# RWKV transposes, inverse levels, chain outputs, softmax and tables in larger steps, and the sample tokens of all eight RWKV heads in one go

## The chip, the cores and the metric

One core of one Trainium2 chip runs the kernel. The metric is the device time of one execution in microseconds (us). Engines are named as in the profile: PE is TensorE (PEld its weight loads), DVE is VectorE, ACT is ScalarE, POOL is GpSimd and SP is SyncE, which here only starts DMAs.

## The reference, cut to what matters

One inference step of one decoder layer for 256 prompt tokens and 32 sample tokens (8 sequences of 4), so 288 tokens (NT) of width 2048, all in float32:

```
h = RMSNorm_pre(x);  [p_rwkv | lru_x | lru_gate | q | k | v] = h @ W_in
y = concat(RWKV7(p_rwkv), RGLRU(lru_x, lru_gate), DilatedWindowAttn(q, k, v)) @ W_out
x = x + RMSNorm_post(y)
x = x + RMSNorm_post2(relu(RMSNorm_pre2(x) @ W1)^2 @ W2)
```

RWKV7 has 8 heads of 64 features; per token `S = S*w + (S·(-kk))(kk*a)^T + v k^T`, `y = S·r`, and behind it a normalisation over each head (here `gen_gn`), a bonus term and a gate. RG-LRU is a gated linear recurrence over 512 features. Attention has 8 heads of 128; the sample tokens attend to a cache of 2048 positions, of which the dilated windows use 896 (keys `kc`, values `vc`). Outputs are the new x of all tokens, the RWKV states, the shift rows, the LRU states and the new keys and values.

## The kernel before, in words

**The main matmuls.** W_in is 46 tiles of 128 columns, each against 16 blocks of 128 features; W_out is 16x16 such blocks, and W1 and W2 of the feed-forward part (FFN) 64x16 each. A product with a 128x128 block is `mm3` (L428): three matmuls of 128x128 weights against 288 columns, high part by high part (L429), high by the low part of x (L430), low part of the weight by high (L431). That makes 9120 of them, called *mains* here, and a position in the program is given as the number of mains before it. Weights come as chunks of 512 KB (8 blocks, 24 mains) on SP's queue; ACT writes the high part into `ring_h` (L393), DVE the low part into `ring_l` (L394), and each ring has 3 places.

**The side work.** Everything else (RWKV, LRU, attention) is written as Python generators that are advanced a bit after each chunk (`pump`, with a budget of some us of estimated PE time), so their matmuls and transposes stand in small *batches* between the mains of W_in and W_out. A `yield` ends a step; each engine then runs its instructions in the order in which a scheduler sets them, and it is this order that the change moves. Small matmuls write one of five PSUM banks (`bt`) that are asked for with `bk(n)`. Temporary tiles come from an arena (`aw`, tiles named `ar` and `arx` in the trace), as soon as a place is free.

**RWKV** works on halves `hf` of 4 heads: decay and key preparation (`gen_rwkv`), transposes to token rows (`gen_tok`, L791), products within chunks of 64 tokens (`gen_form`, L815), a triangular inverse by levels (`gen_inv` on DVE, L855/L857, and `gen_mats` once for each 128 tokens `j`: L898, L911, L912, and L928 behind it), the chain over chunks (`gen_chain`: L964, L975, L986, L987, L1002, L1003, L1013), the sample tokens (`gen_rwkv_sample(hf)`, L1049 to L1123), and the normalisation (`gen_gn`: L1138, L1145, two reciprocals L1150, L1151, L1154, L1156, gate L1161), which waits for chain and sample of its half.

**Attention.** `gen_tables` makes bias tables (L1356), `gen_sample_scores` multiplies queries with cached keys (L1409; query tiles by POOL in L1390 and L1393; loads of 896 KB in L1377), softmax is on DVE (L1434), its transposes are L1447, and `gen_sample_pv` multiplies with cached values (L1496, one batch of 28 matmuls of 128x32 weights for each of 2x8 pairs; loads of 1024 and 768 KB in L1474; copies out by L1503). `gen_prompt_attn` (L1547, bias loads by POOL; L1567, L1588) does the prompt. Key and value loads go into *streams*: buffers for one load each, on POOL's queue, in the order in which POOL's instructions stand. Two streams lie in `arm`; `more_streams` adds up to two from the arena once the second RWKV half has its tiles.

Of the kernel before, what the change touches and what calls it, by code (L numbers as in the profile page):

```python
# [311 lines left out]
def build(tc, A, O):  # L312
    nc = tc.nc
    sy, dv, ac, po, pe = nc.sync, nc.vector, nc.scalar, nc.gpsimd, nc.tensor
    with ExitStack() as ctx:
# [227 lines left out]
        lora = arena.get(2, 512)  # L543
# [22 lines left out]
        def gen_prenorm():  # L566
# [12 lines left out]
            sy.dma_start(out=lora, in_=A["lora"].rearrange("p (a b) -> p a b", a=2))  # L579
# [81 lines left out]
        def gen_rwkv(hf):  # L661
# [6 lines left out]
            for f in range(2):  # L668
# [3 lines left out]
                pe.matmul(out=b0[:, :NT], lhsT=lora[0:64, 0, fs], rhs=mw[0:64], start=True, stop=True)  # L672
                pe.matmul(out=b1[:, :NT], lhsT=lora[64:128, 0, fs], rhs=mw[64:128], start=True, stop=True)
# [3 lines left out]
                yield 1.0  # L677
            half_up(LW, -0.5 * CDEC)
# [59 lines left out]
            gens.append(gen_tok(R, "B", BK[:, 0]))  # L738
            gens.append(gen_tok(R, "K", BK[:, 1]))
# [27 lines left out]
            gens.append(gen_tok(R, "V", MV))  # L767
# [6 lines left out]
            gens.append(gen_rwkv_sample(hf, SC, Vs))  # L774
# [11 lines left out]
        def gen_tok(R, name, src):  # L786
            for j in range(2):
                t = yield from aw(256, top=True)
                b, = yield from bk(1)
                for f in range(2):  # L790
                    pe.transpose(b[:, 128 * f:128 * f + 128], src[:, f, 128 * j:128 * j + 128], ident)  # L791
                ac.activation(out=t, in_=b[:, 0:256], func=AF.Copy)
                banks.put(b)
                R[name + str(j)] = t
                yield 0.25
# [79 lines left out]
        def gen_mats(hf, j):  # L875
            R = RS[hf]
            while "MA%d" % j not in R:
                yield 0
            MT = R["MA%d" % j]
            i64 = cbv("i64")  # L880
            i64b = i64.unsqueeze(1).to_broadcast([128, 4, 64])
# [4 lines left out]

            rc = (slice(0, 64), slice(64, 128))
            XT = yield from aw(4, 64, top=True)
            Gp = yield from aw(4, 64, top=True)
            dv.tensor_tensor(out=XT, in0=MT[:, :, 0], in1=lvl(4), op=ALU.mult)  # L890
# [136 lines left out]
        def gen_rwkv_sample(hf, SC, Vs):  # L1027
            R = RS[hf]
            AR, BK, PS = SC[:, 0], SC[:, 1], R["PS"]
            while "Q0" not in R:  # L1030
                yield 0
# [821 lines left out]
```

## Time and profile before

| | before |
|---|---|
| median of 3 runs | 1447.4 us (1447.09 to 1448.56) |
| profiled execution, its time | 1447.71 us |
| its span | 1445.6 us |
| mean granted TensorE clock | 0.989 |
| PE busy | 1412.0 us (98%) |
| DVE busy | 836.5 us (58%) |
| ACT busy | 600.2 us (42%) |
| POOL busy | 63.3 us (4%) |
| DMA | 276.62 MB, mean 191 GB/s |

W_in and W_out with all side work fill the first 600 us, the FFN the rest. Of the chain of work that ended last, 82% is PE, 7% issue, 6% DMA, 4% DVE and 1% POOL. PE is busy nearly throughout, so its average over the span says little of single stretches; they are read one by one.

### The profile page before, as it was taken

The numbers are of one execution on the slowest core, as the hardware profiler recorded it, in microseconds if no ns is written. First come the engines' busy times: TensorE is split into PE (matmuls) and PEld (weight loads), VectorE is DVE, ScalarE is ACT, GpSimd is POOL, SyncE is SP. The second block draws the span as 40 slices with busy tenths as digits, with TensorE's granted clock in tenths as the row PEclk, the third lists the DMA queues.
The fourth block names the chain that finished last, engine by engine and source line by source line (L and its number), as shares of the span: only waits on it lengthen the run. The fifth ranks groups of instructions, "written<-read, shape, count | busy, mean of one in ns | idle before, by whom it ended". The sixth has DMA issues, their size and how long they took to land.

```text
span 1445.6 us, 27979 instructions
## 1 busy us (share of the span) xinstructions
PE 1412.0 (98%) x11730; PEld 1340.2 (93%) x11730; DVE 836.5 (58%) x1431; ACT 600.2 (42%) x870; POOL 63.3 (4%) x127
## 2 busy tenths in 40 slices
PE   8999999899999999999999999999999999999995
PEld 8899778777878999999999999999999999999995
DVE  7796476645686756795533455544455444555555
ACT  7433422333352533664433344333344333444442
POOL 2101010210001100000000000000000000000000
PEclk9999999999999999999999999999999999999998
DMA  8546566676678774344444444444444445444442
GB/s 299 181 152 209 187 240 239 223 271 241 217 292 331 290 286 162 131 148 161 170 164 165 170 162 163 172 161 167 169 161 165 171 161 169 167 161 165 171 162 79
DMA packets 86047, 276.62 MB, mean 191 GB/s; under 512 B 22385, under 2 KB 26017, under 8 KB 83873
## 3 DMA queue, kind: packets, MB, share of 16 engines
q1 hardware_dynamic: 75136, 212.23, 42.6%
q0 software_dynamic: 9920, 60.83, 11.2%
q8 instruction: 92, 1.51, 0.4%
q10 hardware_dynamic: 864, 1.77, 0.4%
q14 instruction: 35, 0.28, 0.1%
HBM read 267.97 MB, written 6.84 MB: 190 GB/s over the span
## 4 chain that ended last, share of the span: by engine, by line
PE 82%; issue 7%; DMA 6%; DVE 4%; POOL 1%; ACT 0%; SPq 0%; POOLq 0%; DVEq 0%; ACTq 0%
PE mm L429 25%; PE mm L431 25%; PE mm L430 25%; DMA arm<-in_vc 2%; DMA arm<-in_kc 2%; PE bt L1409 1%; DVE ring_l L394 1%; PE bt L1496 1%; DMA ar<-in_vc 1%; DMA w<-in_w_in 0%; DVE arm L1830 0%; DMA do<-ar 0%; DVE arx L1831 0%; DVE hl L548 0%; PE bt L898 0%
## 5 line engine op out<-in xcount | busy, mean ns | idle before, releaser
L394 DVE TENSOR_TENSOR ring_l<-w,ring_h 128x1024 fp32r<-128x1024 f32 (+1 forms) x382 | 464.9, 1218 | 385.2 <-ACT ring_h L393 382.7
L393 ACT ACTIVATE ring_h<-w 128x1024 fp32r<-128x1024 f32 (+1 forms) x382 | 402.6, 1055 | 587.2 <-PE mm L430 538.9
L429 PE MATMUL mm<-hh,ring_h 128*128 128x288 f32 x1984 | 599.4, 302 | 4.6 <-ACT ring_h L393 2.8
L431 PE MATMUL mm<-hh,ring_l 128*128 128x288 f32 x1984 | 591.9, 299 | 1.3 <-DVE ring_l L394 1.3
L430 PE MATMUL mm<-hl,ring_h 128*128 128x288 f32 x1984 | 592.9, 299 | 0.0
L429 PEld LDWEIGHTS mm<-hh,ring_h 128*128 128x128 f32 x1984 | 373.6, 188 | 20.1 <-issue 11.8
L431 PEld LDWEIGHTS mm<-hh,ring_l 128*128 128x128 f32 x1984 | 374.9, 189 | 9.7 <-issue 4.3
L430 PEld LDWEIGHTS mm<-hl,ring_h 128*128 128x128 f32 x1984 | 374.6, 189 | 6.4 <-issue 3.5
L430 PE MATMUL mm<-fl,ring_h 128*128 128x288 f32 x1024 | 302.1, 295 | 0.0
L431 PE MATMUL mm<-fh,ring_l 128*128 128x288 f32 x1024 | 301.8, 295 | 0.0
L429 PE MATMUL mm<-fh,ring_h 128*128 128x288 f32 x1024 | 300.3, 293 | 0.0
L429 PEld LDWEIGHTS mm<-fh,ring_h 128*128 128x128 f32 x1024 | 192.5, 188 | 0.0
L430 PEld LDWEIGHTS mm<-fl,ring_h 128*128 128x128 f32 x1024 | 192.5, 188 | 0.0
L431 PEld LDWEIGHTS mm<-fh,ring_l 128*128 128x128 f32 x1024 | 192.4, 188 | 0.0
L1798 ACT ACTIVATE fh<-ft 128x288 fp32r<-128x288 f32 x64 | 28.3, 445 | 78.9 <-DVE ft L1797 78.9
L1806 DVE TENSOR_TENSOR arm<-mm,arm 128x288 f32<-128x288 f32 x48 | 22.0, 458 | 51.1 <-PE mm L431 51.1
L1799 DVE TENSOR_TENSOR fl<-ft,fh 128x288 fp32r<-128x288 f32 x64 | 29.2, 458 | 29.1 <-ACT fh L1798 29.1
L1409 PE MATMUL bt<-arm,ar 128*32 128x448 f32 x256 | 27.8, 546 | 1.7 <-DMA arm<-in_kc 1.7
L1797 DVE SCALAR_TENSOR_TENSOR ft<-mm,rt 128x288 f32<-128x288 f32 x63 | 28.3, 450 | 0.0
L1496 PE MATMUL bt<-arm,ar 128*32 128x128 f32 x648 | 22.6, 287 | 3.5 <-DMA arm<-in_vc 3.5
L1796 ACT ACTIVATE rt<-mm 128x288 f32<-128x288 f32 x63 | 24.9, 395 | 0.4 <-PE mm L431 0.4
L1496 PEld LDWEIGHTS bt<-arm,ar 128*32 128x32 f32 x648 | 17.8, 114 | 6.6 <-DVE ar L1290 3.7
(394 smaller groups left out, 898.6 us busy)
## 6 DMA issues: line engine op xcount, KB each, us to landing
w<-in_w SPq DMA_DIRECT2D x256, 512.0 KB
w<-in_w_in SPq DMA_DIRECT2D x91, 512.0 KB
arm<-in_kc POOLq DMA_DIRECT2D x32, 896.0 KB, 6.1
w<-in_w_out SPq DMA_DIRECT2D x32, 512.0 KB
arm<-in_vc POOLq DMA_DIRECT2D x15, 1024.0 KB, 6.8
ar<-in_vc POOLq DMA_DIRECT2D x9, 768.0 KB, 9.5
arm<-in_vc POOLq DMA_DIRECT2D x7, 768.0 KB, 7.0
arx<-in_xT SPq DMA_DIRECT2D x6, 576.0 KB
```

Of the source, the lines that this page charges most:

```text
L393: ac.activation(out=h[:, lo:hi], in_=t[:, lo:hi], func=AF.Copy)
L394: dv.tensor_tensor(out=l[:, lo:hi], in0=t[:, lo:hi], in1=h[:, lo:hi].bitcast(F32), op=ALU.subtract)
L429: pe.matmul(out=ps, lhsT=h, rhs=xh, start=start, stop=False)
L430: pe.matmul(out=ps, lhsT=h, rhs=xl, start=False, stop=False)
L431: pe.matmul(out=ps, lhsT=l, rhs=xh, start=False, stop=stop)
L1409: pe.matmul(out=bh[32 * h:32 * h + 32, 0:448], lhsT=qz[:, h, b], rhs=t[:, h], start=(b == 0), stop=(b == NB - 1))
L1496: pe.matmul(out=bb[32 * h:32 * h + 32, 0:128], lhsT=PT[:, kt, 32 * h:32 * h + 32], rhs=t[:, q, h], start=(kt == 0), stop=(kt == 6))
L1796: ac.activation(out=r, in_=ps, func=AF.Relu)
L1797: dv.scalar_tensor_tensor(out=f, in0=ps, scalar=0.0, in1=r, op0=ALU.max, op1=ALU.mult)
L1798: ac.activation(out=fh[:, m], in_=f, func=AF.Copy)
L1799: dv.tensor_tensor(out=fl[:, m], in0=f, in1=fh[:, m].bitcast(F32), op=ALU.subtract)
L1806: dv.tensor_tensor(out=facc[:, m], in0=ps, in1=facc[:, m], op=ALU.add)
```

## The change

- `gen_tok` transposes both 128-token blocks of a tile into one bank, and B and K in one step with two banks.
- `gen_mats` handles both blocks `j` at once: 8 groups to a bank, so 16 matmuls of 64x64 (or 32, L924 and L925) stand together, with copies and DVE operations of 512 columns.
- In `gen_chain` the products into `bZ` (L1013) move up to those into `be` (L964), and are now L984 and L978; ACT copies them to Y at once, and DVE adds the rest later.
- `gen_rwkv_sample` runs once, for 4 feature tiles (8 heads), after both halves. So both calls of `gen_gn` wait for the same sample step.
- Tables and softmax transposes take two banks in one step.
- The streams in `arm` shrink from 2304 to 2048 columns; the 512 columns left become a third piece of the arena. Some tiles are freed earlier (`lora_in`, `mw`, `AR`, `PC`), and the LRU outputs become four tiles. `gen_lru` now stands first in the list.

```diff
-        arena = Arena([arx, ar1])
+        arena = Arena([arx, ar1, arm[:, 4096:4608]])
-        streams = [arm[:, 0:2304], arm[:, 2304:4608]]
+        streams = [arm[:, 0:2048], arm[:, 2048:4096]]
...
-            gens.append(gen_tok(R, "B", BK[:, 0]))
-            gens.append(gen_tok(R, "K", BK[:, 1]))
+            gens.append(gen_tok(R, ("B", BK[:, 0]), ("K", BK[:, 1])))
...
-            gens.append(gen_rwkv_sample(hf, SC, Vs))
+            R["SC"], R["Vs"] = SC, Vs
+            if hf:
+                gens.append(gen_rwkv_sample())
...
+            bs = yield from bk(len(pairs))
+            for i, ((name, src), b) in enumerate(zip(pairs, bs)):
+                for j in range(2):
+                    for f in range(2):
+                        o = 256 * j + 128 * f
+                        pe.transpose(b[:, o:o + 128], src[:, f, 128 * j:128 * j + 128], ident)
...
-        def gen_mats(hf, j):
+        def gen_mats(hf):
...
             for l in range(4, 6):
                 b, = yield from bk(1)
-                for h in range(4):
+                for h in range(8):
                     for r in rc:
-                        pe.matmul(out=v4(b)[r, h], lhsT=XT[r, h], rhs=T[r, h], start=True, stop=True)
-                dv.tensor_tensor(out=Gp, in0=v4(b), in1=i64b, op=ALU.add)
+                        pe.matmul(out=v8(b)[r, h], lhsT=XT[r, h], rhs=T[r, h], start=True, stop=True)
+                dv.tensor_tensor(out=Gp, in0=v8(b), in1=i64b, op=ALU.add)
...
-                for h in range(4):
+                for h in range(8):
                     for r in rc:
                         if l < 5:
-                            pe.matmul(out=v4(bT)[r, h], lhsT=Q[r, h], rhs=Gp[r, h], start=True, stop=True)
-                        pe.matmul(out=v4(bQ)[r, h], lhsT=Gp[r, h], rhs=Q[r, h], start=True, stop=True)
+                            pe.matmul(out=v8(bT)[r, h], lhsT=Q[r, h], rhs=Gp[r, h], start=True, stop=True)
+                        pe.matmul(out=v8(bQ)[r, h], lhsT=Gp[r, h], rhs=Q[r, h], start=True, stop=True)
...
+                    bZ, = yield from bk(1)
+                    for f in range(2):
+                        for e in range(2):
+                            re = slice(64 * e, 64 * e + 64)
+                            pe.matmul(out=bZ[re, 64 * f:64 * f + 64], lhsT=Z[re, f], rhs=AR[re, 1, f, tok],
+                                      start=True, stop=True)
...
+                    ac.activation(out=Y[:, :, tok], in_=v2(bZ), func=AF.Copy)
...
-        def gen_rwkv_sample(hf, SC, Vs):
+        def gen_rwkv_sample():
+
+            while not all("Q0" in R and "SC" in R for R in RS):
+                yield 0
...
-            while "Y" not in R:
+            while not all("Y" in R for R in RS):
                 yield 0
             b, = yield from bk(1)
-            for f in range(2):
+            for f in range(4):
...
+            for hf in range(2):
+                ac.activation(out=RS[hf]["Y"][:, :, tk], in_=v4(b, 32)[:, 2 * hf:2 * hf + 2], func=AF.Copy)
+                RS[hf]["Ys"] = True
...
             for g in range(2):
-                for lo, n in ((0, 464), (464, 464)):
-                    b, = yield from bk(1)
+                bs = yield from bk(2)
+                for b, lo, n in ((bs[0], 0, 464), (bs[1], 464, 464)):
...
-        gens += [gen_tables(), gen_lora()]
+        gens += [gen_lru(), gen_tables(), gen_lora()]
         for hf in range(2):
-            gens += [gen_rwkv(hf), gen_form(hf), gen_inv(hf), gen_mats(hf, 0), gen_mats(hf, 1), gen_chain(hf), gen_gn(hf)]
-        gens += [gen_lru()]
+            gens += [gen_rwkv(hf), gen_form(hf), gen_inv(hf), gen_mats(hf), gen_chain(hf), gen_gn(hf)]
```

**PE, the last inverse level of the first half.** Around main 916 of the kernel before, the two token blocks have a batch of 8 each at L912:

```order
L429 MATMUL mm<-hh,ring_h 128x288
L912 MATMUL bt<-ar_88 64x64 x8
L430 MATMUL mm<-hl,ring_h 128x288
L431 MATMUL mm<-hh,ring_l 128x288
L429 MATMUL mm<-hh,ring_h 128x288
L430 MATMUL mm<-hl,ring_h 128x288
L912 MATMUL bt<-ar_88 64x64 x8
L431 MATMUL mm<-hh,ring_l 128x288
```

In the changed kernel, around main 908, the same work (now L925) and what follows it (L928, now L940, beside key matmuls L1438) read:

```order
L430 MATMUL mm<-hl,ring_h 128x288
L925 MATMUL bt<-ar_88 64x64 x16
L431 MATMUL mm<-hh,ring_l 128x288
L429 MATMUL mm<-hh,ring_h 128x288
L430 MATMUL mm<-hl,ring_h 128x288
L431 MATMUL mm<-hh,ring_l 128x288
L429 MATMUL mm<-hh,ring_h 128x288
L430 MATMUL mm<-hl,ring_h 128x288
L1438 MATMUL bt<-arm,ar_88 32x448 x8
L940 MATMUL bt<-ar_88 64x64 x16
```

Two batches of 8 became one of 16, with the same matmuls in it. In all, PE has 198 small batches before and 162 after, of which 118 and 92 hold tiles smaller than 128x128.

**DVE, the normalisation.** In the kernel before, the first half's reciprocals (L1150) stand behind the low part of a weight chunk (L394), among the inversion steps of the second half (L855, L857) and the sample state (L1121, L1123):

```order
L394 TENSOR_TENSOR ring_l<-w_2306,ring_h 128x1024
L1150 RECIPROCAL ar_88<-ar_88 128x288
L855 TENSOR_TENSOR ar_88<-ar_88 64x1
L1121 TENSOR_TENSOR ar_88<-bt,ar_88 128x512
L857 TENSOR_REDUCE ar_88<-ar_88 64x1
L1150 RECIPROCAL ar_88<-ar_88 128x288
L855 TENSOR_TENSOR ar_88<-ar_88 64x4
L1123 TENSOR_TENSOR ar_88<-ar_88 128x512
L857 TENSOR_REDUCE ar_88<-ar_88 64x2
L1151 TENSOR_TENSOR ar_88<-ar_88 128x576
```

In the changed kernel nothing of `gen_gn` stands there. It stands near main 1900, between the low parts of two successive chunks (L1177 is the reciprocal, L1178, L1181 and L1183 the operations behind it, L1148 and L1149 the sample state, L1528 a copy of attention, L1210 and L1211 of an LRU input). The first part of it:

```order
L394 TENSOR_TENSOR ring_l<-w_3863,ring_h 128x1024
L1166 SCALAR_TENSOR_TENSOR ar_88<-bt,ar_88 128x288
L1303 SCALAR_TENSOR_TENSOR ar_88<-ar_88 128x288
L1210 TENSOR_TENSOR arx<-mm,rs_in 128x256
L1211 TENSOR_TENSOR arx<-mm,rs_in 128x32
L1177 RECIPROCAL ar_88<-ar_88 128x288 x3
L1178 TENSOR_TENSOR ar_88<-ar_88 128x576
L1528 SCALAR_TENSOR_TENSOR arx<-bt,ca,arx 128x128
```

and what follows directly, up to the next low part:

```order
L1181 TENSOR_SCALAR ar_88<-ar_88,pv 128x288 x2
L1177 RECIPROCAL ar_88<-ar_88 128x288
L1183 TENSOR_TENSOR ar_88<-ar_88 128x576
L1178 TENSOR_TENSOR ar_88<-ar_88 128x576
L1148 TENSOR_TENSOR ar_88<-bt,ar_88 128x512
L1181 TENSOR_SCALAR ar_88<-ar_88,pv 128x288 x2
L1149 TENSOR_TENSOR ar_88<-ar_88,arm 128x512
L1183 TENSOR_TENSOR ar_88<-ar_88 128x576
L1148 TENSOR_TENSOR ar_88<-bt,ar_88 128x512
L394 TENSOR_TENSOR ring_l<-w_3943,ring_h 128x1024
```

Both halves' normalisations, four reciprocals, now stand in one stretch between two low parts.

**POOL, the value loads.** In the kernel before, the first value loads of the run (L1474) go to the two `arm` streams in turn, and an arena tile (`ar`) joins late:

```order
L1474 DMA arm<-in_vc 128x2048
L1474 DMA arm<-in_vc 128x1536
L1474 DMA arm<-in_vc 128x2048
L1474 DMA arm<-in_vc 128x1536
L1474 DMA ar_88<-in_vc 128x2048
L1474 DMA arm<-in_vc 128x2048
L1474 DMA arm<-in_vc 128x1536 x2
```

In the changed kernel the same loads (L1499) go round four streams from their start:

```order
L1499 DMA arm<-in_vc 128x1536
L1499 DMA ar_88<-in_vc 128x2048
L1499 DMA arx<-in_vc 128x1536
L1499 DMA arm<-in_vc 128x2048
L1499 DMA arm<-in_vc 128x1536
L1499 DMA ar_88<-in_vc 128x2048
L1499 DMA arx<-in_vc 128x1536
L1499 DMA arm<-in_vc 128x2048
```

A load into a stream waits for the batch that read the load four places before, no longer two.

## Rows read from the trace of the kernel before

**Rows 1.** Windows: busy us (count) per engine, granted clock, DMA share, GB/s.
```profile
0.00:600.40 600.40, 584.32 (x5519) 513.60 (x5520) 409.90 (x919) 250.57 (x403) 63.32 (x127) 0.99 0.66 236
609.50:1428.00 818.50, 818.50 (x6152) 817.99 (x6153) 411.24 (x490) 345.14 (x458) 0.00 (x0) 1.00 0.47 161
```

**Rows 2.** Timeline of PE, a batch of 16 small matmuls: start, duration, instruction.
```profile
302.06 0.29 PE L431 MATMUL mm<-hh,ring_l 128*128 128x288 f32 x1
302.28 0.68 PE L912 MATMUL bt<-ar 64*64 64x64 f32 x16
302.89 0.41 PE L429 MATMUL mm<-hh,ring_h 128*128 128x288 f32 x1
303.13 0.30 PE L430 MATMUL mm<-hl,ring_h 128*128 128x288 f32 x1
```

**Rows 3.** Timeline of PE, a batch of 32 small matmuls.
```profile
289.40 0.29 PE L431 MATMUL mm<-hh,ring_l 128*128 128x288 f32 x1
289.61 0.34 PE L911 MATMUL bt<-ar 64*64 64x64 f32 x4
...
290.74 0.40 PE L429 MATMUL mm<-hh,ring_h 128*128 128x288 f32 x1
290.98 0.30 PE L430 MATMUL mm<-hl,ring_h 128*128 128x288 f32 x1
```

**Rows 4.** Timeline of PE, a batch of four 128x128 transposes.
```profile
384.49 0.60 PE L1447 MATMUL bt<-ca,arx 128*128 128x128 f32 x4
384.84 0.38 PE L429 MATMUL mm<-hh,ring_h 128*128 128x288 f32 x1
385.06 0.30 PE L430 MATMUL mm<-hl,ring_h 128*128 128x288 f32 x1
```

**Rows 5.** Timeline of DVE between two low parts.
```profile
242.67 1.95 DVE L1150 RECIPROCAL ar<-ar 128x288 f32<-128x288 f32 x1
244.54 0.09 DVE L855 TENSOR_TENSOR ar<-ar 64x1 f32<-64x1 f32 x1
...
256.38 1.21 DVE L394 TENSOR_TENSOR ring_l<-w,ring_h 128x1024 fp32r<-128x1024 f32 x1
```

**Rows 6.** Timeline of PE; in brackets the idle time before and what ended it.
```profile
256.50 0.25 PE L1421 MATMUL bt<-ar,arx 128*32 128x32 f32 x2 [0.97 <-DVE ar L1316]
...
279.00 0.96 PE L1409 MATMUL bt<-arm,ar 128*32 128x448 f32 x8 [1.73 <-DMA arm<-in_kc]
```

**Rows 7.** Timeline of POOL, same columns.
```profile
267.61 1.08 POOL L1547 DMA_DIRECT2D ar<-dtab  x2 [27.21 <-ACT ar L1449]
...
274.25 1.06 POOL L1377 DMA_DIRECT2D arm<-in_kc  x2
```

**Rows 8.** Windows around the waits of PE, columns as in Rows 1.
```profile
253.20:282.00 28.80, 24.66 (x202) 19.93 (x200) 20.55 (x54) 11.42 (x22) 8.17 (x10) 0.94 0.56 175
423.60:459.40 35.80, 31.11 (x377) 27.30 (x376) 26.07 (x69) 13.67 (x22) 4.77 (x9) 0.90 0.91 340
258.10:261.50 3.40, 3.40 (x14) 2.97 (x12) 2.85 (x7) 2.00 (x6) 0.00 (x0) 0.50 0.49 154
432.20:439.00 6.80, 5.57 (x65) 4.69 (x65) 1.50 (x4) 1.13 (x2) 0.53 (x1) 0.50 0.85 319
```

**Rows 9.** Timeline of POOL, the load that PE waits for next.
```profile
424.98 1.19 POOL L1474 DMA_DIRECT2D arm<-in_vc  x2 [11.37 <-PE bt L1496]
```

**Rows 10.** Timeline of PE, that wait.
```profile
433.43 0.87 PE L1496 MATMUL bt<-arm,ar 128*32 128x128 f32 x12 [3.54 <-DMA arm<-in_vc]
```

**Rows 11.** Windows before that load and from its issue to its landing.
```profile
400.00:425.00 25.00, 25.00 (x250) 21.72 (x253) 20.76 (x31) 14.79 (x20) 1.61 (x4) 1.00 0.70 272
424.98:433.43 8.45, 4.91 (x47) 4.51 (x38) 8.01 (x17) 5.36 (x7) 1.06 (x2) 0.92 0.98 351
```

**Rows 12.** Groups of DVE by line: count, busy us, mean ns of one.
```profile
L1154 DVE TENSOR_SCALAR ar<-ar,pv 128x288 f32<-128x288 f32 x4 | 1.6, 421 | 0.0
L1156 DVE TENSOR_TENSOR ar<-ar 128x576 f32<-128x576 f32 x2 | 1.5, 747 | 0.0
```

More of the change, by code (lines that the diff above doesn't have):

```diff
@@ new lines, in gen_rwkv_sample @@
+            BK = [RS[f // 2]["SC"][:, 1, f % 2] for f in range(4)]
+            Z0 = []
+            for hf in range(2):
+                Z0.append((yield from aw(2, NB, 64, top=True)))
+                po.dma_start(out=Z0[hf], in_=A["wkv0"][:, 2 * hf:2 * hf + 2])
+            z0 = lambda f: Z0[f // 2][:, f % 2]
+            SM = yield from aw(4, 64, top=True)
+            AZ = yield from aw(4, 64, top=True)
+            UV = yield from aw(4, 64, top=True)
+            BKT = yield from aw(4, 128, top=True)
@@ new lines, in gen_rwkv_sample @@
+            banks.put(b)
+            for hf in range(2):
+                for e in range(2):
+                    dv.tensor_copy(out=TM[:, 2 * hf:2 * hf + 2, 64 * e:64 * e + 64].rearrange("p f (k t) -> p f k t", k=2),
+                                   in_=RS[hf]["SC"][:, 1])
+            yield 0.7
+            b, = yield from bk(1)
+            for f in range(4):
+                pe.transpose(b[:, 128 * f:128 * f + 128], TM[:, f], ident)
+            ac.activation(out=BKT, in_=v4(b, 128), func=AF.Copy)
@@ L1126, in gen_rwkv_sample @@
-            sy.dma_start(out=O["o_wkv_s"][:, 2 * hf:2 * hf + 2], in_=Z0)
-            arena.put(Z0, SM, AZ, UV, BKT, Ab, SC, Vs)
-            R["Zs"] = True
+            yield 0.6
+            Ab2 = yield from aw(512, top=True)
+            for hf in range(2):
+                PS = RS[hf]["PS"]
+                A2 = (Ab, Ab2)
+                for f in range(2):
+                    dv.tensor_tensor(out=A2[f].rearrange("p (b v) -> p b v", b=NB),
+                                     in0=UV[:, 2 * hf + f].unsqueeze(1).to_broadcast([128, NB, 64]), in1=m8, op=ALU.mult)
+                yield 0
+                bs = yield from bk(2)
+                for f in range(2):
+                    for e, re in enumerate(halves_):
+                        pe.matmul(out=bs[f][re], lhsT=BKT[re, 2 * hf + f, 64 * e:64 * e + 64], rhs=A2[f][re], start=True, stop=True)
+                    z = Z0[hf][:, f]
+                    dv.tensor_tensor(out=z, in0=bs[f].rearrange("p (b v) -> p b v", b=NB), in1=z, op=ALU.add)
+                    dv.tensor_tensor(out=z, in0=z, in1=PS[:, f].unsqueeze(2).to_broadcast([128, NB, 64]), op=ALU.mult)
+                banks.put(*bs)
+                yield 1.8
+                sy.dma_start(out=O["o_wkv_s"][:, 2 * hf:2 * hf + 2], in_=Z0[hf])
+                arena.put(Z0[hf], RS[hf]["SC"], RS[hf]["Vs"], PS)
@@ L1227, in gen_lru @@
                 yield 0
[L1228 removed]
+            S["LY"] = []
             hfin = yield from aw(4)
```

255 lines of the change are left out of this document (112 added, 143 removed).

## The prediction

> **What bounds the kernel now.** I read three things in this order: windows by stage, the timeline of PE, and the timelines of the engines that PE waits for. The windows split the span in two [rows 1]. In the FFN (609.5 to 1428 us) PE is busy for all of 818.5 us with 6152 instructions, 0.133 us each; no edit touches that, and it is no use to look there. In the first 600.4 us PE stands idle for only 16.1 us. The FFN has 6144 of the 9120 mains, so 2976 lie here: 2976 x 0.133 = 395.8 us. What is left of the busy time, 584.3 - 395.8 = 188.5 us, are the 190-odd small batches of side work, about 1 us apiece. So the change can win in two ways: cheaper batches, or fewer waits of PE with what hangs on them.
>
> A batch costs more than its matmuls. In [rows 2] one main starts at 302.06, then 16 matmuls of 64x64 tiles, and the second main behind them starts at 303.13: 1.07 us, of which two mains are 0.27, so the batch costs 0.80. In [rows 3] a batch of 32 runs from 289.40 to 290.98: 1.58 - 0.27 = 1.31. Sixteen more matmuls cost 0.51, or 0.032 each, so 0.29 of each batch is fixed: the main ahead of it takes 0.21 to 0.22 until the batch starts where 0.133 is usual, the main behind it 0.24, and the rest lies inside. A batch of four full 128x128 transposes [rows 4] costs 0.57 - 0.13 = 0.44, which is 0.11 each with nothing fixed in sight.
>
> The waits are in two stretches. In 253.2 to 282.0, PE is idle 28.80 - 24.66 = 4.1 us, and in 423.6 to 459.4 it is idle 35.80 - 31.11 = 4.7 us [rows 8]. [...] The stretches lose 5.8 and 7.5 us.
>
> **The change part by part.** *Fewer batches.* The order of PE's instructions has the same small matmuls in 162 batches instead of 198; of those with tiles smaller than 128x128 there are 92 instead of 118. At 0.30 (the 0.29 of the rows, rounded up since the batches of four and eight that I priced in the same way leave 0.32): 26 x 0.30 = **-7.8**. Bounds: if only the entry and exit, 0.20 together, are saved, -5.2; with 0.32, -8.3. The other ten are batches of full tiles: nothing, by [rows 4]. The wider copies and adds that belong to them (512 columns instead of two of 256) are on DVE and ACT, at 68% and 42% of the first 600 us [rows 1], and I cost them at nothing where PE has other mains to run; where it has not, the last term stands for it.
>
> *The first stretch.* Between two low parts of weight chunks DVE has 13.7 us of other work [rows 5], from 242.67 to 256.38, two reciprocals of 1.95 in it. PE runs dry at 256.50 (0.97) and again just after, and softmax on DVE gets late too. Then ACT's softmax step is late for POOL: a bias load waited 27.21 us for it, and behind it stood the query tiles and a key load, issued only at 274.25 [rows 7], which PE waits for until 279.00 (1.73) [rows 6]. In the changed order the first half's `gen_gn` is gone from here, the query tiles stand ahead of the bias loads, and a third stream lets one more key load run ahead. The load that follows is due some 8.7 us after its issue, against 4.75 from 274.25 to 279.00. I keep 0.8 of 5.8 for the softmax transposes, now in one step: **-5.0** (bounds -2.5, if half of it stays because DVE still does the inversion and softmax there, and -5.8).
>
> *The second stretch.* The load that PE waits for at 433.43 could not start before 424.98, since its buffer came free only then [rows 9, 10]. Before it, from 400 to 425 us, DMA was at 0.70 and 272 GB/s; from its issue to its landing it was at 0.98 and 351 [rows 11]. The changed order has four streams from the first value load on, so a load waits for the batch four loads back. Batches five to eight now stand at mains 1990, 2015, 2026 and 2058. Batch seven's loads start when batch five ends: 36 mains, batch six and the sample step between give about 9.1 us, against 8.45 for the two of [rows 9 to 11]; batch eight has 8.7 us. By volume: two pairs of loads (3.67 MB) and weights for 68 mains (1.5 MB) at 351 GB/s are 14.7 us, and up to main 2058 PE needs 9.0 for the mains and about 8 for the two value batches and the sample and attention steps. So it fits, closely: 1.0 of wait is left. **-6.5** (bounds 0, if the loads merely share a full DMA, and -7.5).
>
> *The new pile.* What left the first stretch comes back near main 1920. Both halves' normalisations now stand between two low parts on DVE: four reciprocals 4 x 1.95 = 7.8 [rows 5], four operations of 576 columns and three of 512 (0.75 and, in proportion, 0.66) 5.0, four of 0.42 [rows 12] 1.7, three small ones of attention and LRU 0.9, the low part itself 1.2 [rows 5]: 16.6. Neighbours overlap by 0.08 (242.67 + 1.95 against 244.54 [rows 5]), 18 times, so 15.2, and 0.3 to reach PE: 15.5 us, counted from the LRU tile that L1210 waits for, at main 1871. PE has to have the low part 52 mains later, 6.9 us, with seven batches between that take 6.3 by the same pricing: 13.2. The queue on DVE is fixed, so the low part and all mains behind it wait: **+2.3** (bounds 0, if PE is late there for another reason, and 3.8, without overlap). After waits of 2 us in short pieces the trace shows 3.4 us at half clock, after one of 3.5 us 6.8 us [rows 8]; a wait of 2.3 lies near the first: **+1.7** (0 to 3.4).
>
> *Steps that wait for two inputs.* A joined batch needs both its inputs, and its successor both copies: the levels stand six mains (0.8 us) apart, while a copy out of PSUM of 512 columns and the add behind it take longer than before. The trace shows no such joined step. Some ten places look tight; at 0.15 each **+1.5** (0 to 3). The moved `bZ` matmuls, earlier frees of tiles and the LRU's place add no work, and with ACT and DVE no busier I cost them at nothing.
>
> Sum: -7.8 - 5.0 - 6.5 + 2.3 + 1.7 + 1.5 = -13.8. The profiled execution took 1447.7, so 1433.9; the median of the runs is 0.3 below the profiled one, so **1433.6 us**.
>
> **The rivals.** *B, the value loads are bound by rate.* [Rows 11] speaks for it: in the 8.45 us of that load DMA was busy 0.98. Then a third and fourth load in flight only share what one pair had, the wait comes back at batch seven or eight, and the 6.5 are lost: **1440.1**. Against it: 0.70 in the 25 us before, which four streams can fill. [...]
>
> *C, the joined steps give nothing.* Each of the 26 joined batches then waits as long for its later input as the fixed 0.30 saves (-7.8 gone), and three of these waits bring half clock as after the first stretch (3 x 1.7 = 5.1): 1433.6 + 12.9 = **1446.5**. For it: 6 mains between levels. Against it: in the kernel before the levels stand as close, and PE's idle time outside the two stretches is 16.1 - 4.1 - 4.7 = 7.3 us in all.
>
> *D, slower: value loads starve the weights.* With up to four loads in flight, weights get a smaller part of about 351 GB/s. A chunk is used in some 4.7 us (24 mains 3.2, half a value batch 0.9, other batches 0.6; an estimate), so it needs 512 KB / 4.7 us = 111 GB/s, 32% of the rate. From main 1750 to 2424 there are 28 chunks. The change turns into a loss when each is 13.8 / 28 = 0.5 us late, which is a share of 29%; at 27%, 5.5 us per chunk, 28 x 0.8 = 22 us are lost: **1456**. Against it: with DMA at 0.98, PE waited for a value load and no weight.
>
> **How the numbers follow.** The forecast gets 0.60: its terms rest on rows, two of them (batches and first stretch) on plain counts. B gets 0.22, C 0.10, D 0.08. Around the forecast, the bounds of the terms give about 1427 (all large: -8.3 - 5.8 - 7.5 + 0.5 with few new waits) to 1438; B adds up to 1442, and both together hold over 8 in 10: 1427 to 1442. A difference of 0.2%, 2.9 us, is about what a measurement of this kernel can tell from none. Faster: the forecast, B and a little of C, 0.84; the same: the rest of C, 0.08; slower: D, 0.08.
>
> **What the changed profile would show.** Batches: PE's busy time in the first 600 us down by about 8, and a batch of 32 at L925 still at 1.3. First stretch: no wait of PE above 1 us for L1438 or for a low part between 250 and 285 us, and no granted clock of 0.5 there. Second: the value loads of L1499 issued two batches ahead, DMA above 0.70 before 425 us, waits at L1521 below 1 us together. New pile: a wait of 2 to 3 us for `ring_l` near 400 us, three L1177 in a row ahead of it on DVE, some us of clock 0.5 behind. I am wrong if L1521 waits by 3 us or more at batch seven or eight (B), if many small waits stand behind copies of ACT or adds of DVE at L924, L925, L997 or L978 (C), or if PE waits for `ring_h` with `w` late (D).

## The result, and the profile after

The changed kernel takes 1439.3 us (median of 7 runs, 1436.8 to 1445.1), the kernel before 1447.4. The ratio is 0.9946, with a 95% interval of 0.9929 to 0.9964: 8.1 us faster, where 13.8 were forecast. The profiled execution took 1438.5 us, its span is 1436.7 (before: 1445.6), so 8.9 us of span are to be explained.

The page of the changed kernel, parts 1 (busy time of each engine) and 4 (the chain that ended last):

```profile
PE 1399.8 (97%) x11730; PEld 1335.7 (93%) x11730; DVE 834.6 (58%) x1411; ACT 595.5 (41%) x857; POOL 57.4 (4%) x127
...
PE 73%; DVE 1%; DMA 1%; ACT 1%; issue 0%; DVEq 0%
```

PE was busy for 1412.0 us before, so 12.2 us of its work are gone, more than the span lost. Part of the gain was given back as waiting. The windows of the changed kernel (columns as in [rows 1]) show where:

```profile
0.00:591.40 591.40, 571.98 (x5517) 508.94 (x5518) 407.84 (x898) 245.96 (x389) 57.39 (x127) 0.99 0.69 240
180.00:400.00 220.00, 209.94 (x2175) 173.56 (x2174) 128.14 (x303) 71.75 (x132) 25.27 (x50) 0.98 0.74 260
256.50:262.90 6.40, 3.42 (x13) 3.24 (x14) 2.77 (x9) 0.00 (x0) 0.00 (x0) 0.50 0.42 112
250.90:259.30 8.40, 2.33 (x15) 1.97 (x14) 1.54 (x5) 1.06 (x1) 0.21 (x1) 0.81 0.82 279
400.00:425.00 25.00, 23.46 (x190) 19.46 (x190) 24.36 (x33) 10.43 (x14) 1.06 (x2) 1.00 0.46 157
430.00:460.00 30.00, 28.49 (x376) 24.41 (x373) 26.27 (x70) 10.18 (x19) 4.22 (x8) 1.00 1.00 385
```

The stretch around the second value loads, which lost 7.5 us before (4.7 idle and half of the 5.57 busy at a granted clock of 0.50 [rows 8]), loses 1.5 (30.00 - 28.49) at full clock. But from 180 to 400 us PE idles for 10.1 us, and for 6.4 us the granted clock is 0.50: a main then starts every 0.24 us (261.17, 261.41, 261.65), where at full clock it is 0.13 (263.02, 263.15, 263.29). PE's timeline has the places:

```profile
237.26 0.51 PE L781 MATMUL bt<-ar,ca 128*128 128x288 f32 x1 [2.80 <-DVE ar L782]
...
251.55 0.49 PE L1588 MATMUL bt<-arx 128*128 128x128 f32 x2 [0.58 <-DVE arx L1526]
...
259.49 0.79 PE L1588 MATMUL bt<-arx 128*128 128x128 f32 x2 [5.68 <-DVE ar L1592]
...
289.41 1.15 PE L925 MATMUL bt<-ar 64*64 64x64 f32 x32
290.49 0.40 PE L429 MATMUL mm<-hh,ring_h 128*128 128x288 f32 x1
...
412.36 0.40 PE L429 MATMUL mm<-hh,ring_h 128*128 128x288 f32 x1 [0.75 <-ACT ring_h L393]
...
414.69 0.51 PE L1282 MATMUL bt<-arx 128*128 128x288 f32 x1 [0.79 <-DVE ar L1148]
...
447.60 0.86 PE L1521 MATMUL bt<-arx,ar 128*32 128x128 f32 x24 [1.51 <-DMA arx<-in_vc]
```

Two waits are new: 2.80 us at L781 and 5.68 at L1588, the score matmul of the prompt's attention. Both end on DVE, and the clock of 0.50 stands where the prediction expected none (its sign was no granted clock of 0.5 between 250 and 285 us). DVE's own rows say what it waited for:

```profile
236.51 0.15 DVE L864 TENSOR_TENSOR ar<-ar 64x1 f32<-64x1 f32 x1 [3.31 <-DMA o_k<-arx]
...
236.77 0.44 DVE L782 TENSOR_TENSOR ar<-bt,ar 128x288 f32<-128x288 f32 x1
...
252.51 0.29 DVE L1592 SCALAR_TENSOR_TENSOR ar<-bt,arx 128x128 f32<-128x128 f32 x1 [1.01 <-PE bt L1589]
...
259.00 0.42 DVE L1592 SCALAR_TENSOR_TENSOR ar<-bt,arx 128x256 f32<-128x256 f32 x1 [5.84 <-DMA do<-ar]
```

L864 is the first operation of `gen_inv`, the inversion of the 16x16 diagonal blocks, which runs on DVE. `gen_inv` rearranges its blocks by two trips through DRAM: it writes them to `dm` (L852) and reads them back per block (L858, eight loads), inverts on DVE, writes the results to `do` (L872) and reads those back (L877). These are the second half's trips on SP's queue:

```profile
217.24 4.66 SPq L852 DMA_DIRECT2D dm<-ar  x2
...
229.59 2.91 SPq L858 DMA_DIRECT2D ar<-dm  x8
...
250.90 1.29 SPq L872 DMA_DIRECT2D do<-ar  x2
...
259.29 2.78 SPq L877 DMA_DIRECT2D ar<-do  x6
```

The same trips in the kernel before (not among the rows ahead of the prediction):

```profile
225.71 6.70 SPq L843 DMA_DIRECT2D dm<-ar  x2
...
236.09 2.86 SPq L849 DMA_DIRECT2D ar<-dm  x8
...
268.83 1.57 SPq L863 DMA_DIRECT2D do<-ar  x2
...
272.14 3.53 SPq L868 DMA_DIRECT2D ar<-do  x6
```

The read-back waits for its write to land: DVE's L1592, which waits for the write to `do`, starts at 259.00, the read-back is issued at 259.29, and in the run e9 below the rows of the two read-backs name `dm<-ar` (7.03 us) and `do<-ar` (1.70) as what they waited for. The first trip takes 19.3 us until DVE can start (217.24 to 236.51; the row names an output on the same queue as releaser, which is inferred, but what L864 reads is what L858 loads, and in the run e1 below the same row names `ar<-dm`). On DVE L782, which needs nothing of the trip, stands behind L864 (236.77 behind 236.51), and PE's L781 waits for L782 (done at 237.21, L781 starts at 237.26). In the kernel before, the first half's normalisation stood there: its first reciprocal, L1150, runs from 242.67, and the inversion starts right behind it at 244.54 without a wait [rows 5]. If the rest of the trip took the 6.9 us that it took in the changed kernel (229.59 to 236.51), it ended near 243.0 there (236.09 + 6.9; an estimate), under that reciprocal. The change moved the normalisation away.

The second trip's write takes 8.4 us from issue to read-back (250.90 to 259.29), against 3.3 before. Its source is the work tile `W`, which `gen_inv` gives back to the arena as soon as the write is issued (`arena.put(W)`). In the changed order the score tile `P` of L1592 is laid on it, so DVE waits for the write: its row starts at 259.00, just ahead of the read-back. POOL's queue shows what the write ran beside, two key loads of 896 KB each issued just ahead of it (DMA share 0.82 and 279 GB/s in that window):

```profile
249.88 0.54 POOL L1406 DMA_DIRECT2D arm<-in_kc  x1 [5.83 <-PE bt L1521]
250.57 0.53 POOL L1406 DMA_DIRECT2D arm<-in_kc  x1 [0.15 <-issue]
```

In the kernel before, the next key load was issued at 274.25 [rows 7], behind that write.

### The profile page after: what moved, and what is told of

The parts are those of the page before. It is cut to its first block, busy times and chain, and to the rows that moved or that the text cites. A ratio compares the mean times of both kernels' runs of the same rounds, so it can differ in the third digit from the quotient of the medians.

```text
span 1436.7 us, 27941 instructions
## 1 busy us (share of the span) xinstructions
PE 1399.8 (97%) x11730; PEld 1335.7 (93%) x11730; DVE 834.6 (58%) x1411; ACT 595.5 (41%) x857; POOL 57.4 (4%) x127
## 3 DMA queue, kind: packets, MB, share of 16 engines
q0 software_dynamic: 9920, 60.83, 11.7%
q8 instruction: 92, 1.51, 0.4%
## 4 chain that ended last, share of the span: by engine, by line
PE 73%; DVE 1%; DMA 1%; ACT 1%; issue 0%; DVEq 0%
PE mm L429 23%; PE mm L430 23%; PE mm L431 23%; PE bt L1521 1%; DMA arx<-in_vc 1%; DVE arm L1854 0%; DVE arx L1855 0%; PE bt L1146 0%; PE bt L425 0%; ACT ring_h L393 0%; PE bt L1115 0%; DVE ring_l L394 0%; PE mm L412 0%; PE bt L429 0%; PE bt L1165 0%
## 5 line engine op out<-in xcount | busy, mean ns | idle before, releaser
L394 DVE TENSOR_TENSOR ring_l<-w,ring_h 128x1024 fp32r<-128x1024 f32 (+1 forms) x382 | 465.0, 1218 | 388.2 <-ACT ring_h L393 381.2
L429 PE MATMUL mm<-hh,ring_h 128*128 128x288 f32 x1984 | 597.3, 301 | 5.2 <-ACT ring_h L393 3.3
L431 PE MATMUL mm<-hh,ring_l 128*128 128x288 f32 x1984 | 589.7, 298 | 0.2 <-DVE ring_l L394 0.2
L429 PEld LDWEIGHTS mm<-hh,ring_h 128*128 128x128 f32 x1984 | 373.4, 188 | 17.0 <-issue 8.5
L431 PEld LDWEIGHTS mm<-hh,ring_l 128*128 128x128 f32 x1984 | 374.6, 189 | 9.2 <-issue 6.3
L431 PE MATMUL mm<-fh,ring_l 128*128 128x288 f32 x1024 | 301.9, 295 | 0.0
L429 PE MATMUL mm<-fh,ring_h 128*128 128x288 f32 x1024 | 300.3, 293 | 0.0
L429 PEld LDWEIGHTS mm<-fh,ring_h 128*128 128x128 f32 x1024 | 192.5, 188 | 0.0
L431 PEld LDWEIGHTS mm<-fh,ring_l 128*128 128x128 f32 x1024 | 192.4, 188 | 0.0
L1438 PE MATMUL bt<-arm,ar 128*32 128x448 f32 x208 | 23.2, 546 | 1.3 <-DMA arm<-in_kc 1.0
L1729 DVE TENSOR_TENSOR ar<-mm,ar 128x288 f32<-128x288 f32 x32 | 14.5, 454 | 11.4 <-PE mm L431 11.4
L1406 POOL DMA_DIRECT2D arm<-in_kc x26 | 13.7, 528 | 98.3 <-PE bt L1438 90.8
```

What stands on the lines that cost most here:

```text
L394: dv.tensor_tensor(out=l[:, lo:hi], in0=t[:, lo:hi], in1=h[:, lo:hi].bitcast(F32), op=ALU.subtract)
L429: pe.matmul(out=ps, lhsT=h, rhs=xh, start=start, stop=False)
L431: pe.matmul(out=ps, lhsT=l, rhs=xh, start=False, stop=stop)
L1438: pe.matmul(out=bh[32 * h:32 * h + 32, 0:448], lhsT=qz[:, h, b], rhs=t[:, h], start=(b == 0), stop=(b == NB - 1))
L1729: dv.tensor_tensor(out=macc(m), in0=ps, in1=macc(m), op=ALU.add)
```

## The experiments

All were timed beside the kernel before, whose median in the three groups was 1446.3, 1445.8 and 1445.6 us. Four theories are at stake. The reused tile: the 5.68 us are a matter of where `P` lies. The cover: what is missing is the first half's normalisation in the first stretch, under which the trips ran before. The trip itself: the DRAM trips are late whatever stands around them; it was formed after the first group of runs. And for the value loads, buffers against rate (rival B of the prediction).

**The tile held** (e1_hold_tile, from the changed kernel): `W` is given back only when the inverse is done.

```diff
-            arena.put(W)
             for _ in range(3):
                 yield 0
             R["TQ"] = TQ
+            while "Q0" not in R:
+                yield 0
+            arena.put(W)
```

> The changed kernel, but the work tile of the inversion goes back to the arena only when the inverse is finished, so that the score tile of the prompt attention can't be laid on it while its two 64 KB writes to DRAM are under way. PE has the same 162 batches. Theory 1 (reused tile): the 5.7 us wait of PE at L1588 and the 3.4 us of busy time at half clock behind it (1.7 lost) vanish, so 7.4 us below the changed kernel: about 1432 (1430 to 1434). Theory 2 (the side work of this stretch is late anyway, and the write only ended last): the wait comes back at another tile or another engine within 2 us: 1437 to 1440. The wait of 2.8 us at L781 stays by either.

Measured: 1439.35 us, ratio 0.9945 [0.993, 0.996], the same as the changed kernel. PE's timeline of this run:

```profile
239.79 1.33 PE L781 MATMUL bt<-ar,ca 128*128 128x288 f32 x2 [5.98 <-DVE ar L782]
...
269.40 0.30 PE L912 MATMUL bt<-ar 64*64 64x64 f32 x2 [1.01 <-DMA ar<-do]
...
271.18 1.12 PE L912 MATMUL bt<-ar 64*64 64x64 f32 x16 [1.48 <-DMA ar<-do]
```

The wait of 5.68 is gone, as meant, and the time stayed: 5.98 us are now waited for the first trip and 2.5 for the read-back of the second. The expectation's second branch, a wait that comes back elsewhere, held. Holding the tile is not worth the wait it removes. The run is no clean test, though: bias loads and the arena moved with it, and the first trip took 22.4 us (216.61 to 239.04) instead of 19.3. What the tile costs when the write is short is seen in e7 and e9 below.

**The sample tokens per half again** (e2_split_sample, from the changed kernel), which brings the first half's normalisation back into the first stretch:

```diff
-            R["SC"], R["Vs"] = SC, Vs
-            if hf:
-                gens.append(gen_rwkv_sample())
+            gens.append(gen_rwkv_sample(hf, SC, Vs))
...
-        def gen_rwkv_sample():
+        def gen_rwkv_sample(hf, SC, Vs):
```

> The changed kernel with the sample tokens done again for each half by itself, as before the change; the first normalisation is free to go back to the first stretch. 174 batches, 103 with small tiles, instead of 162 and 93. By the shifted arena the score tile no longer lies on the inversion's tile. Theory 1 (reused tile): -7.4 for that wait, -1.5 for the late pile of both normalisations, +3.0 for ten batches, and 0 to +4 of DVE pile and kc waits back in the first stretch: 1433 to 1438. Theory 3 (the joint normalisation is what cost the missing 5 us, the reused tile is chance): the 2.8 wait at L781 goes too, since DVE is no longer early at the inversion, and about 1433 or below.

Measured: 1457.84 us, ratio 1.0072 [1.0055, 1.0088], slower than both kernels. The waits of PE by what it waited for (us in total, times, longest):

```profile
PE bt L908 <- DMA ar<-do: 9.9, 2, 8.4
...
PE bt L1425 <- DMA arm<-in_kc: 3.3, 3, 2.2
...
PE bt L1175 <- DVE arx L1515: 1.8, 1, 1.8
```

There is no wait for the first trip. But that isn't the normalisation's doing: on DVE the inversion starts ahead of its first reciprocal, behind softmax work of the attention.

```profile
239.81 0.14 DVE L862 TENSOR_TENSOR ar<-ar 64x1 f32<-64x1 f32 x1
...
243.85 1.94 DVE L1164 RECIPROCAL ar<-ar 128x288 f32<-128x288 f32 x1
```

Then the second trip costs 8.4 us at one place, where two value loads were issued just ahead of its write (9.29 us from issue to read-back). Both expectations missed, and the theory of the cover is not confirmed. The edit also adds 12 batches and changes the order behind them, so how much of the 18.6 us over the changed kernel belongs to the sample step alone stays open.

**Two streams for the value loads** (e3_two_streams, from the changed kernel):

```diff
-NSTR, LAG = 2, 3
+NSTR, LAG = 0, 3
```

> The changed kernel with no stream from the arena: two buffers for key and value loads instead of four. By the shifted arena the score tile no longer lies on the inversion's tile. If value loads start late for want of buffers (the forecast's term): -7.4 for the reused tile, and PE waits at most of the batches seven to sixteen for 1 to 5 us, 12 to 20 us in all with half clock: 1444 to 1452. If the loads are bound by rate and four streams only share it: waits as in the changed kernel, about 1.5 us, so 1432 to 1434.

Measured: 1459.46 us, ratio 1.0083 [1.0062, 1.0104]; its profiled execution was its fastest, 1452.2. Its waits:

```profile
PE bt L1521 <- DMA arm<-in_vc: 8.3, 8, 3.5
PE bt L1438 <- DMA arm<-in_kc: 4.2, 3, 2.2
```

Waits for value loads are 8.3 us instead of 1.5. With four streams the DMA engines moved 385 GB/s from 430 to 460 us; here it is 313 in the same stretch and 336 around the longest wait (438 to 450 us), and the kernel before had 351 around its own [rows 11]. More loads in flight did bring bandwidth: buffers were the limit, rival B falls. The loss is larger than expected; waits for key loads (4.2 us, 1.0 in the changed kernel) are part of it.

**Only the inverse joined** (e4_only_inverse, from the kernel before): `gen_mats` for both blocks at once, 186 batches of small matmuls instead of 198.

```diff
-        def gen_mats(hf, j):
+        def gen_mats(hf):
...
-                for h in range(4):
+                for h in range(8):
                     for r in rc:
-                        pe.matmul(out=v4(b)[r, h], lhsT=XT[r, h], rhs=T[r, h], start=True, stop=True)
+                        pe.matmul(out=v8(b)[r, h], lhsT=XT[r, h], rhs=T[r, h], start=True, stop=True)
```

> The kernel before with one part of the change alone: the inverse levels and the products behind them for both token blocks at once. 186 batches instead of 198, 106 instead of 118 with small tiles, same matmuls. If a batch with small tiles has a fixed 0.30 us: 12 x 0.30 = 3.6 us less, if the order of waits stays as it was: 1443.8 (1442 to 1446). If joined steps wait for the later input as much as they save: 1446 to 1449, with new waits of PE behind ACT copies or DVE adds of the levels.

Measured: 1440.61 us, ratio 0.9958 [0.9945, 0.9972]: 5.6 us for 12 fewer batches, more than expected. PE's busy time fell by 6.0 us (1412.0 to 1406.0). What PE lost at half clock has to be taken off both: 7.9 us before (4.5 in the two stretches, 3.4 near 605 us) and 6.7 here, by the windows of both traces. That leaves 4.8 us, or 0.40 per batch, somewhat more than the 0.30 priced. The rest is waits that moved: the value load now costs 0.7, and a key matmul (L1414) waits 2.0 for a query tile that POOL copies (L1398).

**No trip, changed and before** (e5_hold_no_trip, which holds the tile too, and e6_before_no_trip): the read-backs of the second half load from an input instead of from `dm` and `do`, so they wait for no write. The second half's inverse then doesn't depend on its data.

```diff
-            d = dm[0:1, 0:1]
+            d = A["wkv0"][0:1, 0:1, 0, 0:1] if hf else dm[0:1, 0:1]
...
-                d = do[cb_:cb_ + 1, 0:1, 0:1]
+                d = do[cb_:cb_ + 1, 0:1, 0:1] if not hf else A["wkv0"][16 * cb_:16 * cb_ + 1, 0:1, 0, 0:1]
```

> The kernel with the held work tile, and in the second half the two read-backs of the inversion (blocks in, inverse out) take their data from an input in DRAM instead of what was just written there. So this kernel leaves out the dependence of the second half's inverse on its own data; the same transfers are issued, with the same sizes, and need not wait for a write. PE and DVE run in nearly the same order as with the held tile. Theory 4 (the inversion's two trips through DRAM take 20 and 13 us beside weight and key loads, and what had covered them was moved away): the waits at L781 (5.98) and at the first inverse level (1.01 and 1.48) go, with the half clock behind both (1.8 and 3.0): 1426 to 1430. Theory 2 (the side work of this stretch is late anyway): 1436 to 1440, with PE waiting for DVE in the same places.

> The kernel before, with the same two read-backs of the second half taken from an input (same part left out). Theory 4: before the change the trips were covered, by the first half's normalisation on DVE above all, and PE waited for neither in the second half: 1445 to 1447.5. If the trips cost as much before the change as after it: 1434 to 1440.

Measured: 1426.81 us, ratio 0.9864 [0.9851, 0.9877], and 1441.57 us, ratio 0.997 [0.9958, 0.9982]. The window from 180 to 400 us of the changed kernel without the trip:

```profile
180.00:400.00 220.00, 219.59 (x2291) 181.92 (x2290) 139.12 (x316) 76.00 (x137) 26.34 (x52) 1.00 0.76 267
```

Of 220 us PE idles 0.4, where it idled 10.1. Against the run with the tile held, 12.5 us are gained (1439.35 - 1426.81; 11.7 by the two ratios). That is an upper bound on the price of the trips, since this kernel does more than make them short: with no data to wait for, the second half's inversion runs on DVE from 193.85 to 206.58 us, ahead of the first trip's write at 217.26, so its own 13 us have left the full stretch too. In the kernel before 4.2 us are gained, though no wait of PE there names the trips; DVE in that run (e6) shows why:

```profile
226.28 0.15 DVE L855 TENSOR_TENSOR ar<-ar 64x1 f32<-64x1 f32 x1
...
240.54 0.38 DVE L860 COPY ar<-ar 64x256 f32<-64x256 f32 x1
...
243.38 1.95 DVE L1150 RECIPROCAL ar<-ar 128x288 f32<-128x288 f32 x1
```

The whole inversion is done at 240.5, ahead of the reciprocals, and between 240 and 300 us PE has no wait at all. So it was the late trip that pushed the inversion into the pile of [rows 5]. Here it starts at 226.28, just behind the issue of the first write (225.73), which is nearer to a trip that takes no time. The expectation of next to no gain in the kernel before missed; that of the changed kernel held. Without the trip the change is worth 14.8 us (1441.57 - 1426.81), close to the forecast of 13.8, though the two kernels compared don't have the inversion in the same place.

**The trips on POOL's queue** (e7_trip_on_pool with the tile held, e9_pool_alone without, both from the changed kernel; e10_before_pool from the kernel before). All four transfers of the second half's trips are changed alike:

```diff
             R = RS[hf]
+            qe = po if hf else sy
...
-                sy.dma_start(out=dm[:, 256 * j:256 * j + 256].rearrange("p (h t) -> p h t", h=4), in_=R["MA%d" % j][:, :, 0])
+                qe.dma_start(out=dm[:, 256 * j:256 * j + 256].rearrange("p (h t) -> p h t", h=4), in_=R["MA%d" % j][:, :, 0])
```

> The held tile, and the second half's trips issued on POOL's queue instead of SP's; nothing is left out. Key and value loads then stand behind the trips on POOL, and the trips no longer behind weight loads on SP. Theory 4 (the trips are long because loads are in flight with them and ahead of them): the first trip ends some us earlier, the wait at L781 falls from 6 to below 3, 1433 to 1436, if the key loads that are held up don't bring waits of their own at L1440 (each would add about 2). If the trips are long by themselves: 1439 or above.

> The changed kernel with the second half's trips on POOL's queue, without the held tile: the score tile of the prompt attention still lies on the inversion's work tile and waits for its write to DRAM. Theory 4 (the write took 8 us only because key loads had been issued just ahead of it): on POOL the key loads stand behind it, it lands in some 3 us, and the wait at L1588 shrinks from 5.7 to below 1.5; the wait behind the first trip shrinks to about 2.5 as with the held tile: 1432 to 1435. If the reuse of the tile is a cause by itself: 1437 to 1440.

> The kernel before with the second half's trips on POOL's queue. Leaving the dependence out gave 4.2 us there, so theory 4 has at most that to gain, and key loads behind the trips may cost one wait: 1442 to 1446. If POOL's queue is worth 7 us whatever the kernel (something else than the trips): 1438 to 1440.

Measured: 1432.12 us, ratio 0.9905 [0.989, 0.9919]; 1432.06, ratio 0.9904 [0.9881, 0.9927]; 1453.99, ratio 1.0058 [1.0042, 1.0074]. The first two beat both kernels, the changed one by 7 us (6 by the ratios). POOL's rows with the tile not held:

```profile
251.76 1.20 POOL L873 DMA_DIRECT2D do<-ar  x2 [7.52 <-DVE arx L1527]
252.96 0.58 POOL L1407 DMA_DIRECT2D arm<-in_kc  x1
255.24 3.91 POOL L878 DMA_DIRECT2D ar<-do  x7 [1.70 <-DMA do<-ar]
```

The write now stands ahead of the key load on the same queue and takes 3.5 us to the read-back, not 8.4. Queue and order changed together here, but SP's queue in e1, where the key loads came behind the write (259.19), tells them apart:

```profile
255.14 1.28 SPq L872 DMA_DIRECT2D do<-ar  x2
258.09 4.39 SPq L877 DMA_DIRECT2D ar<-do  x8
```

That is 2.95 us, so SP's queue by itself doesn't make the write long. Where it is long (8.05 to 9.76 us), two large loads were issued within 2 us of it (all traces are in the last section). With the tile held or not, the time is the same within the spread of the runs: once this write is short, the reused tile costs nothing that shows. The first trip did not get shorter, which e7's expectation had counted on (20.2 us in e9, 22.5 in e7); with the tile held DVE still waits for it, and so does PE:

```profile
240.02 0.33 PE L1453 MATMUL bt<-ar,arx 128*32 128x32 f32 x6 [2.60 <-DVE ar L782]
```

In the kernel before the same move loses 8 us, which neither theory had. The timelines of POOL and of PE there:

```profile
269.51 1.18 POOL L864 DMA_DIRECT2D do<-ar  x2 [0.53 <-issue]
...
273.82 0.59 POOL L1378 DMA_DIRECT2D arm<-in_kc  x1
275.38 3.91 POOL L869 DMA_DIRECT2D ar<-do  x7 [0.97 <-issue]
...
283.63 1.72 PE L1410 MATMUL bt<-arm,ar 128*32 128x448 f32 x8 [6.51 <-DMA arm<-in_kc]
```

With two streams, PE already waited 1.73 us for the key load of this place [rows 6]; now bias loads and the trip stand around it on the queue, and PE waits 6.51 us. That the move pays in the changed kernel because its streams let the key loads run further ahead is my reading of these rows; no run varies it alone.

**Only the streams** (e8_only_streams, from the kernel before): the smaller value streams and the 512 columns given to the arena.

```diff
-        arena = Arena([arx, ar1])
+        arena = Arena([arx, ar1, arm[:, 4096:4608]])
...
-        streams = [arm[:, 0:2304], arm[:, 2304:4608]]
+        streams = [arm[:, 0:2048], arm[:, 2048:4096]]
```

> The kernel before with one part of the change alone: streams of 2048 columns and the third piece of the arena. Same 198 batches. Arena tiles that serve as third and fourth stream are found earlier, but three of the first eight value loads still go to two buffers. If buffers are what value loads wait for: the wait of 3.5 us at L1496 shrinks by half and its half clock goes, 1441 to 1445. If rate binds them: 1446 to 1449.

Measured: 1448.66 us, ratio 1.0019 [1.0007, 1.0032]. Its waits:

```profile
PE bt L1496 <- DMA arm<-in_vc: 2.3, 1, 2.3
PE bt L1409 <- DMA arm<-in_kc: 2.1, 1, 2.1
PE bt L777 <- DVE ar L857: 2.0, 1, 2.0
```

The time lies where the expectation put a limit by rate, but for another reason. The value loads cost 2.3 instead of 3.5 + 1.1 us, and without half clock behind them, but 2.0 us behind the inversion (L857) are new, with 4 us of reduced clock (0.57) after them. The first trip's read-back was issued at 238.22, 2.1 us later than in the kernel before, and DVE waits for it:

```profile
247.53 0.15 DVE L855 TENSOR_TENSOR ar<-ar 64x1 f32<-64x1 f32 x1 [2.48 <-DMA o_k<-ar]
```

The normalisation stands in its old place here, with the first reciprocal directly ahead of this row (243.10 to 245.05), and does not cover the trip. Part of the gain was given back there.

**The inversion behind L782** (e11_pool_bonus_first, from e7): its first operation on DVE is queued behind both L782, so that nothing waits behind the first trip.

```diff
+            while hf and "bv" not in R:
+                yield 0
...
+                if hf and t == 1:
+                    after(first, R["bvi"])
```

> The held tile and the trips on POOL, and the first operation of the second half's inversion made to stand behind the two bonus products on DVE (L782), so that DVE doesn't wait for the first trip ahead of work that PE needs. Nothing is left out. If the 2.6 us wait and the 3 us lost at half clock behind it come from that order on DVE: 1427 to 1430. If DVE then only waits one instruction later, with a weight chunk's low part behind it: 1431 to 1434.

Measured: 1432.13 us, ratio 0.9913 [0.9893, 0.9933], no better than e7. The 2.60 us wait is gone (1.02 are left there, at full clock), but the inversion ends later, and the waits come back behind it, the largest at a value load:

```profile
PE bt L1528 <- DMA arm<-in_vc: 2.5, 1, 2.5
```

## Why the prediction was wrong in size

Direction and range held; the gain came out 5.7 us smaller than forecast. That the range held is in part luck: one term was off by 10 us, and the others by 5.1 in all the other way. For each term, the forecast, and what the two spans show (idle time, and half of the busy time at 0.50, from the rows above and [rows 8]):

- Batches: -7.8 forecast, -9.4 measured (PE's busy time fell by 12.2, of which 2.8 is less time at half clock: 4.5 before, 1.7 after; the 3.4 lost behind W_out are in both). A batch of 32 runs 1.08 from its start to the next main (289.41 to 290.49), 1.13 before [rows 3], so the saving is in their number: 0.36 for each of the 26 here, 0.40 in e4, where 0.30 was priced.
- Value loads: -6.5 forecast, -6.0 measured (1.5 of 7.5 is left). Right, and e3 shows buffers as the reason.
- The new pile: +2.3, and +1.7 for its half clock, forecast; +1.5 measured (0.75 + 0.79), and the clock stayed at 1.00 from 400 to 425. Too dear by 2.5. The 0.3 to reach PE in its sum was the author's estimate, and no run shows it: PE's L431 starts 0.04 us behind the end of the low part that it waits for in the kernel before (257.59 to 257.63), L781 0.05 behind L782 in the changed one (237.21 to 237.26).
- Joined steps: +1.5 forecast, nothing to be seen. The 0.15 a place was the author's estimate, worked out from no row. The wider steps do take longer: ACT's copies out of a bank 596 ns for 512 columns (L929) against 376 for 256 (L916 before), DVE's adds 690 (L911) against 424 (L899 before). But the waits of PE outside the places named differ by less than 1 us in sum. Rival C has nothing for it, nor has D: waits for weights (L429 for `ring_h`) grew from 2.8 to 3.3 us in sum.
- **The first stretch: -5.0 forecast, +5.0 measured**, 10 us off and outside its own bounds of -5.8 to -2.5. The waits are 2.80 + 0.58 + 5.68 = 9.1 us, and half of 3.42 is lost to the clock: 10.8 where 5.8 were lost before (4.1 idle and half of the 3.40 at 0.50 [rows 8]).

The last is the step that failed. It read the pile on DVE as the sum of its rows and took the first half's normalisation out of it. It did not ask why the inversion stood in that pile: it waited for its first trip through DRAM. In the changed order DVE comes to the inversion before the trip has ended, and PE waits behind DVE. Nor did the prediction look at what lies on the memory that a transfer reads from, and so on who waits for the transfer to land. That the loss hangs on the inversion and its trips is shown: without the dependence the same change gives 14.8 us, with it 6.9 (1446.25 - 1439.35, tile held), and e9, which leaves nothing out and only moves the trips to POOL's queue, gets back 6 to 7 of the 10 us.

That it was the moved normalisation that had covered the first trip is argued from the rows of the kernel before and not shown. In e8 the normalisation is in its old place and DVE waits 2.48 us for the trip all the same; in e2 it is back in this stretch, but behind the start of the inversion, which doesn't wait. What decides in these rows is when the trip ends, against whatever DVE has in front of it.

What stays open is how short the first trip (19 to 22 us) could be. Its rows in the changed kernel have three parts. The second of its two writes is issued 4.3 us behind the first (at 221.5, when the other block is ready; in e9 it waits there for DVE's L831). The read-back is issued 8.1 us behind that, with three key loads of 896 KB issued from 218.89 to 220.16 in between the two writes; in the kernel before, where two key loads came 3 us ahead of the second write, this part took 4.1. DVE starts 6.9 us later, with two value loads issued at 229.50 and 232.59. So loads in flight are the suspects here too, but no run put the first trip clear of them: on POOL's queue two key loads stood between its writes as well (218.38 and 219.13 in e9).

Which engine issues the trips makes little difference in these traces: the first trip took 20.2 us on POOL (e9) and 19.3 on SP (the changed kernel), and the second trip's write, where no key or value load was issued just ahead of it, 3.48 on POOL (e9) and 2.95 on SP (e1). In e9 the read-back starts 2.28 us behind the issue of the second 64 KB (252.96 to 255.24).

## What to carry to other kernels

Before work is moved out of a full stretch, look at what the work behind it waits for: if a transfer ends under the moved work, its time can come out as waiting. A wait that vanishes at one place without a gain in time (the tile held) has moved to the next use of the same late thing; to bound its price, take the thing itself away once, in a kernel that leaves out the dependence, and look where the work that hung on it goes. A small transfer on which much depends is put ahead of large loads on their queue, if those loads run far enough ahead to bear the delay (e9 gained 7 us, e10 lost 8; the condition is my reading of the two).

## What was not expected of the hardware

The second trip's write, two times 64 KB, took 2.95 to 3.49 us from its first issue to the read-back in five traces (e1 2.95, before 3.31, e8 3.36 on SP; e9 3.48, e7 3.49 on POOL) and 8.05 to 9.76 in four, all on SP (e4 8.05, the changed kernel 8.39, e2 9.29, e3 9.76). In the four, two key or value loads of 768 to 1024 KB were issued within 2 us of its first issue; in the five, none in the 10 us ahead of it and at most one behind (e9). The busy share of the DMA engines doesn't tell the two apart: it was 0.81 in e8 and 0.82 in the changed kernel. (In e10 and e11 key loads stand between the trip's own transfers on POOL's queue, so their times can't be compared.)

In the changed kernel the granted clock fell to 0.50 at 256.5, in a wait of 5.68 us that ended at 259.49, and stayed there for 6.4 us, to 262.9. After one of 2.60 us (e7) it was 0.54 on average over 7.5, and after one of 1.97 us (e8) 0.57 over 4; after waits of 2.80, 1.51 and 0.79 us in the changed kernel it was 1.00. Length of the wait alone doesn't decide it.
